# Scaled h in place of the normalised input for the first two gate/up blocks of a two-layer diffusion backbone

## The chip, the cores and the metric

The kernel runs on one core of a Trainium2 chip. The metric is the device time of one execution in microseconds. The core has a matrix engine (TensorE, in the profile PE, its weight loads PEld), VectorE (DVE), ScalarE (ACT), GpSimd (POOL), and a queue engine that issues most loads (SyncE, SP). Matrix products end in PSUM, in 8 banks of 128 x 512 numbers; everything else lies in SBUF.

## The reference

Two layers; in each a half-step feed-forward block, a mixer of three head groups, and a second half-step feed-forward block, on 256 latent and 256 context tokens of 1024 channels. The change touches only the first feed-forward block of the first layer:

```python
def rms_norm(x, g):
    return x * rsqrt(mean(x * x, axis=-1) + EPS) * g
def modulate(n, shift, scale):
    return n * (1 + scale) + shift
def swiglu(x, wg, wu, wd):
    return (silu(x @ wg) * (x @ wu)) @ wd
sh1, sc1, gt1, ... = split(silu(c) @ w_ada[l] + b_ada[l], 9)
h = h + 0.5 * gt1 * swiglu(modulate(rms_norm(h, g_ffn1[l]), sh1, sc1), *ffn1)
```

The context tokens pass through the same weights with their own vectors. For a token with r = 1/rms, the input of the first products is h r m + s, with m = g (1 + scale) and s = shift, both by channel and stream. Its product with a weight column w is therefore r (h m) w + s w: the first factor is one number for each token, the last term one number for each hidden unit and stream.

## The kernel before, in words

Channels lie on the 128 partitions (8 row blocks j), the 512 tokens of both streams along the free dimension. Every product is made of three: activations and weights are each cut into a rounded part and the rest (`xh`/`xl`, `whi`/`wlo`), and `mm3` (L348) adds rounded x rounded, rounded x rest, rest x rounded in PSUM. ScalarE makes a rounded part, VectorE the rest.

A feed-forward block (`ffn`, L429) has 22 hidden blocks of 128 units, each with a gate and an up product (two PSUM banks), in groups of 8, 7 and 7; after each group the down product follows. Weights come as tiles of 128 x 2048 in two raw buffers (`raw`), and are cut by halves of 1024 columns into four buffers each of `whi` and `wlo` (`prefetch`, L321). A half's buffer is free again when its last product has read it.

The first two hidden blocks are made together, in `first_norm` (L140 to 241), while the inputs arrive: h (two loads of 1 MB), the adaLN weights for shift and scale of layer 0 (`wada0`, four quarters q of two halves, 1 MB each, L156), and the weights of blocks 0 and 1 (half tiles, L191). Its steps:

- squares of h on ScalarE, added up on VectorE (L182, L184), then `stats` (L370): sums over the partitions by TensorE, 1/rms in ten small VectorE operations, and its broadcast to all partitions by TensorE; a copy to `rb` (L224)
- for each quarter q: `vectors` (L156, L158), products of the padded activation of c and c_ctx (`cpad`) with the quarter's weights, 512 columns wide, in four column groups of the array; `modulation` (L164 to L176): a copy of the rows, four transposes, a sum, the biases, giving shift `m0` and scale `m1` for two row blocks
- for each row block j: `modulate` (L196 to L203): h times 1/rms on VectorE, scale and shift on ScalarE, rounded part, rest
- `products(j)`: 12 matmuls of 512 columns into the four banks of blocks 0 and 1.

Earlier, `start_ada` (L112) loads c and c_ctx as one row, broadcasts them by eight TensorE instructions (L125) and applies SiLU into `cb`, which the later adaLN sums use: 56 of these in this feed-forward block, made by VectorE (L285) between its other work, each with a 512-KB load (L244).

After that, each hidden block is finished by SiLU of the gate (L456), its product with the up sum (L457), and the cut into `hh` and `hl` (L460, L461), and the PSUM banks are free for the block after next.

The order on each engine is fixed when the program is built: a planner goes through the instructions and lets each engine take, of those whose inputs it believes to be ready, the one that stands first in the program. `issue_after` puts an instruction behind another on its engine. On the chip each engine then runs its list in that order, and loads issued by SP wait in its list until their buffer is free.

## Time and profile before

| | |
|---|---|
| median of 3 runs | 1783.59 us (1782.25 to 1783.96) |
| profiled execution | 1782.73 us, span 1781.0 us |
| TensorE busy | 1730.0 us (97%) |
| VectorE busy | 1144.4 us (64%) |
| ScalarE busy | 647.3 us (36%) |
| GpSimd busy | 97.0 us (5%) |
| read from memory | 249.30 MB, 141 GB/s over the span |

The times in rows of the trace are microseconds from the span's start. A row of the timeline has the start, the busy time, the engine, the line, the operation, output and inputs, and how many instructions were merged into it; in brackets stands how long the engine had been idle and who ended that. Records of matmuls overlap, so the distance between two starts is what one costs, not its length. A row of a group has, behind the bar, the busy time and the mean length in ns. A product of this type on unrounded numbers appears as two instructions.

### The profile page before, as it was taken

The page shows a single profiled execution, that of the slowest core. Times are in us where ns is not written, and L with a number is a line of the kernel's source. Part 1 is how long each engine was busy: PE and PEld are TensorE (multiplying, and loading weights), DVE is VectorE, ACT ScalarE, POOL GpSimd, SP SyncE. Part 2 cuts the span into 40 slices and gives each one's busy share as a digit, 9 for nine tenths or more (in the row PEclk, how much of TensorE's full clock was granted, in tenths as well). Part 3 has the DMA queues.
Part 4 walks back from the last instruction along what each step waited for, and adds up shares of the span by engine and source line. Part 5 has one row for each costly group of instructions (what it writes and reads, how often), then busy time and mean ns, then how long its engine had stood idle before and what let it go on. Part 6 is the DMA issues. An engine that isn't in the chain of part 4 may idle for free.

```text
span 1781.0 us, 24848 instructions
## 1 busy us (share of the span) xinstructions
PE 1730.0 (97%) x9940; PEld 1479.8 (83%) x9940; DVE 1144.4 (64%) x2218; ACT 647.3 (36%) x1053; POOL 97.0 (5%) x130
## 2 busy tenths in 40 slices
PE   7999999999999999999999999999999999989999
PEld 3787888889887688888888898888888898789999
DVE  4777688757657868666676375554543577865554
ACT  4422222234336744212222242222222445744443
POOL 0000000011110010000000110000000311010000
PEclk9999999999999999999999999999999999989999
DMA  7755555532211023544444235534442233135553
GB/s 269 296 195 178 177 178 217 179 101 75 96 57 36 25 107 120 176 165 166 154 178 147 90 122 186 170 134 141 148 141 96 76 118 115 46 109 178 184 184 130
DMA packets 47429, 251.95 MB, mean 141 GB/s; under 512 B 5999, under 2 KB 7233, under 8 KB 29521
## 3 DMA queue, kind: packets, MB, share of 16 engines
q1 hardware_dynamic: 47106, 250.26, 40.5%
q8 instruction: 78, 1.28, 0.3%
q14 instruction: 37, 0.30, 0.1%
q0 software_dynamic: 64, 0.10, 0.0%
q10 hardware_dynamic: 144, 0.01, 0.0%
HBM read 249.30 MB, written 1.05 MB: 141 GB/s over the span
## 4 chain that ended last, share of the span: by engine, by line
PE 88%; DVE 7%; ACT 2%; issue 2%; POOL 1%; DMA 0%; POOLq 0%; ACTq 0%; DVEq 0%
PE mm L350 25%; PE mm L351 25%; PE mm L352 25%; PE mm L627 2%; PE mm L628 2%; PE mm L629 2%; PE aux L836 1%; PE aux L829 1%; DVE wlo L336 1%; POOL acc L368 1%; PE aux L561 1%; PE mm L805 1%; PE aux L774 1%; DVE xl L402 1%; PE aux L387 0%
## 5 line engine op out<-in xcount | busy, mean ns | idle before, releaser
L350 PE MATMUL mm<-xh,whi 128*128 128x512 f32 (+1 forms) x1744 | 606.9, 351 | 6.9 <-ACT xh L201 3.4
L351 PE MATMUL mm<-xl,whi 128*128 128x512 f32 (+1 forms) x1744 | 609.9, 350 | 1.2 <-DVE xl L844 1.2
L352 PE MATMUL mm<-xh,wlo 128*128 128x512 f32 (+1 forms) x1744 | 609.7, 350 | 0.0
L336 DVE TENSOR_TENSOR wlo<-raw,whi 128x1024 fp32r<-128x1024 f32 x324 | 389.5, 1204 | 231.7 <-ACT whi L335 230.2
L335 ACT CAST whi<-raw 128x1024 fp32r<-128x1024 f32 x324 | 332.4, 1027 | 561.5 <-PE mm L351 376.3
L350 PEld LDWEIGHTS mm<-xh,whi 128*128 128x128 f32 x1744 | 332.1, 192 | 52.9 <-ACT xh L201 6.4
L351 PEld LDWEIGHTS mm<-xl,whi 128*128 128x128 f32 x1744 | 333.7, 191 | 45.5 <-issue 1.7
L352 PEld LDWEIGHTS mm<-xh,wlo 128*128 128x128 f32 x1744 | 333.5, 191 | 42.8 <-issue 2.2
L350 PE MATMUL mm<-hh,whi 128*128 128x512 f32 (+1 forms) x788 | 271.3, 344 | 0.0
L351 PE MATMUL mm<-hl,whi 128*128 128x512 f32 (+1 forms) x788 | 270.7, 344 | 0.1
L352 PE MATMUL mm<-hh,wlo 128*128 128x512 f32 (+1 forms) x788 | 270.1, 343 | 0.0
L457 DVE TENSOR_TENSOR gs<-gs,mm 128x512 f32<-128x512 f32 (+1 forms) x88 | 54.7, 621 | 188.1 <-ACT gs L456 149.7
L350 PEld LDWEIGHTS mm<-hh,whi 128*128 128x128 f32 x788 | 149.3, 190 | 19.8 <-issue 2.7
L351 PEld LDWEIGHTS mm<-hl,whi 128*128 128x128 f32 x788 | 149.4, 190 | 18.2 <-DVE hl L461 0.4
L352 PEld LDWEIGHTS mm<-hh,wlo 128*128 128x128 f32 x788 | 149.3, 190 | 17.4
L285 DVE CUSTOM_DVE_ANT_0 ada<-ada,cb 128x1024 f32<-128x1024 f32 x128 | 156.0, 1221 | 2.6 <-DMA ada<-wada 0.6
L407 DVE SCALAR_TENSOR_TENSOR h<-mm,mod,h 128x256 f32<-128x256 f32 x216 | 98.5, 479 | 84.3 <-PE mm L352 83.7
L456 ACT ACTIVATE gs<-mm 128x512 f32<-128x512 f32 (+1 forms) x88 | 48.0, 545 | 276.7 <-PE mm L352 272.8
L368 POOL TENSOR_TENSOR acc<-acc,sq 128x256 f32<-128x256 f32 x63 | 58.2, 932 | 1227.2 <-ACT sq L367 1226.0
L285 DVE CUSTOM_DVE_ANT_0 prod<-ada,cb 128x1024 f32<-128x1024 f32 x96 | 117.0, 1219 | 0.0
L627 PE MATMUL mm<-whi,xh 128*128 128x256 f32 x336 | 97.4, 290 | 0.0
L628 PE MATMUL mm<-wlo,xh 128*128 128x256 f32 x336 | 96.8, 288 | 0.0
(176 smaller groups left out, 1438.3 us busy)
## 6 DMA issues: line engine op xcount, KB each, us to landing
raw<-wgu SPq DMA_DIRECT2D x86, 1024.0 KB, 4.8
ada<-wada SPq DMA_DIRECT2D x128, 512.0 KB, 3.9
raw<-wd SPq DMA_DIRECT2D x32, 896.0 KB, 4.6
raw<-wd SPq DMA_DIRECT2D x16, 1024.0 KB, 4.9
raw<-win SPq DMA_DIRECT2D x12, 1024.0 KB, 5.0
a<-wada SPq DMA_DIRECT2D x8, 1024.0 KB, 4.9
raw<-wout SPq DMA_DIRECT2D x8, 1024.0 KB, 4.9
raw<-why SPq DMA_DIRECT2D x6, 1024.0 KB, 4.8
```

Source lines behind the costliest of these rows:

```text
L285: nc.vector.tensor_tensor_reduce(out=prod, in0=w, in1=self.cb[:, s], scale=1.0, scalar=0.0, op0=ALU.mult, op1=ALU.add, accum_out=m[:, s, j ...
L335: nc.scalar.copy(hi[:, :n], raw)
L336: nc.vector.tensor_tensor(out=lo[:, :n], in0=raw, in1=hi[:, :n].bitcast(F32), op=ALU.subtract)
L350: t.matmul(out, whi, xhi, start=start, stop=False)
L351: t.matmul(out, whi, xlo, start=False, stop=False)
L352: t.matmul(out, wlo, xhi, start=False, stop=stop)
L368: nc.gpsimd.tensor_tensor(out=self.acc[s], in0=self.acc[s], in1=sq, op=ALU.add)
L407: return self.nc.vector.scalar_tensor_tensor(out=self.h[:, j, cols], in0=ps[:, c0:c0 + SEQ], scalar=self.mod(l, ch, s, j), in1=self.h[:, j ...
L456: nc.scalar.activation(gs[:, :n], pg[:, :n], AF.Silu)
L457: nc.vector.tensor_tensor(out=gs[:, :n], in0=gs[:, :n], in1=pu[:, :n], op=ALU.mult)
L627: nc.tensor.matmul(out, self.xh[:, kk, t], hi[:, w], start=kk == 0 and i == 0, stop=False)
L628: nc.tensor.matmul(out, self.xh[:, kk, t], lo[:, w], start=False, stop=False)
```

## The change

`first_norm` no longer waits for the root mean square before the products of blocks 0 and 1. It loads the scale half of the first quarter's adaLN weights first (`vectors(1, 0)`), then half of h and the first halves of the weights, and multiplies h by m alone (`gained`), cut into `uh` and `ul`; these go into the products. The squares come behind the second and fourth row block's products, the statistics behind the sixth. Then the shift halves follow; s is cut into two parts (`sh`), and `shifted(j)` multiplies it with the weights of blocks 0 and 1, 8 small matmuls for each row block into a bank of its own (`pb`), added up into `bias`. The ordinary modulation of all row blocks (`modulate`) comes last, for block 2 and those behind it. Blocks 0 and 1 are finished with `rb` and `bias`. `cb` is made by one broadcast load and one activation at the end. The scratch tiles of squares and modulation now lie in the three buffers of the adaLN weights' tag (`ada`), and the pool `first` is open until block 1 is finished.

```diff
-        crow = self.main.tile([P, 2048], F32, tag="raw", name="raw", bufs=2)[0:1].rearrange("p (s d) -> p s d", s=2)
-        nc.sync.dma_start(crow, a["cc"])
-                nc.tensor.matmul(pt, self.ones[0:1, :], crow[:, s, q * 512:(q + 1) * 512], start=True, stop=True)
-                nc.scalar.activation(self.cb[:, s, q * 512:(q + 1) * 512], pt, AF.Silu)
...
+        def vectors(c, q):
+            pt = self.ps("aux")
+            for half in range(2):
+                w = pool.tile([P, 4, 256], F32, tag="a0", name="a0", bufs=4)
+                nc.sync.dma_start(w, a["wada0"][q, half].rearrange("p (g c k) -> p g c k", g=4, c=2)[:, :, c])
+                for g in range(4):
+                    nc.tensor.matmul(pt[g * 32:(g + 1) * 32, :256], cpad[:, half * 4 + g], w[:, g], start=half == 0, stop=half == 1)
+            return pt
...
+        def gained(j):
+            for s in range(2):
+                cols = slice(s * SEQ, (s + 1) * SEQ)
+                nc.scalar.activation(uh[j][:, cols], self.h[:, j, cols], AF.Identity, scale=m1[:, s, j:j + 1])
+                v.scalar_tensor_tensor(out=ul[j][:, cols], in0=self.h[:, j, cols], scalar=m1[:, s, j:j + 1],
+                                       in1=uh[j][:, cols].bitcast(F32), op0=ALU.mult, op1=ALU.subtract)
...
+        def shifted(j):
+            for k in range(4):
+                hi, lo = weight(j, k // 2, k % 2)
+                nc.tensor.matmul(pb[:, 4 * k:4 * k + 4], hi, sh[:, j].rearrange("p w s -> p (w s)"), start=j == 0 and k == 0, stop=False)
+                nc.tensor.matmul(pb[:, 4 * k:4 * k + 2], lo, sh[:, j, 0], start=False, stop=j == ND - 1 and k == 3)
+
+        parts = vectors(1, 0)
+        inputs(0)
+        weights(0)
+        for q in range(4):
+            modulation(1, q, parts)
+            if q == 0:
+                self.prefetch(2, 2)
+            for j in (2 * q, 2 * q + 1):
+                gained(j)
+            if q < 3:
+                parts = vectors(1, q + 1)
+            if q == 0:
+                inputs(1)
+            elif q == 1:
+                weights(1)
+            elif q == 2:
+                parts0 = vectors(0, 0)
+            for j in (2 * q, 2 * q + 1):
+                products(j)
+            if q in (0, 1):
+                squares(q)
+            elif q == 2:
+                v.tensor_tensor(out=accs[0], in0=accs[0], in1=accs[1], op=ALU.add)
+                rbp, _ = self.stats((0, 1), accs[:1])
+                nc.scalar.copy(rb, rbp)
+        pb = self.ps("aux")
+        for q in range(4):
+            modulation(0, q, parts0)
+            if q == 0:
+                self.prefetch(3, 4)
+            if q < 3:
+                parts0 = vectors(0, q + 1)
+            for j in (2 * q, 2 * q + 1):
+                shifted(j)
+            for j in (2 * q, 2 * q + 1):
+                modulate(j)
+        v.tensor_reduce(out=bias, in_=pb[:, :16].rearrange("p (k w s) -> p k s w", k=4, w=2), axis=AX.X, op=ALU.add)
+        nc.sync.dma_start(self.cb, a["cc"].partition_broadcast(P))
+        nc.scalar.activation(self.cb, self.cb, AF.Silu)
...
+                    if first and b < 2:
+                        up = pool.tile([P, 512], F32, tag="gs", name="up")
+                        nc.vector.tensor_tensor(out=gs, in0=pg, in1=rb, op=ALU.mult)
+                        nc.vector.tensor_tensor(out=up, in0=pu, in1=rb, op=ALU.mult)
+                        for s in range(2):
+                            cols = slice(s * SEQ, (s + 1) * SEQ)
+                            nc.scalar.activation(gs[:, cols], gs[:, cols], AF.Silu, bias=bias[:, 2 * b, s:s + 1])
+                            nc.vector.scalar_tensor_tensor(out=gs[:, cols], in0=up[:, cols], scalar=bias[:, 2 * b + 1, s:s + 1],
+                                                           in1=gs[:, cols], op0=ALU.add, op1=ALU.mult)
```

## Rows read from the trace of the kernel before

**Rows 1.** The page: TensorE's busy time, and the chain that ended last.

```profile
PE 1730.0 (97%) x9940; PEld 1479.8 (83%) x9940; DVE 1144.4 (64%) x2218; ACT 647.3 (36%) x1053; POOL 97.0 (5%) x130
...
PE 88%; DVE 7%; ACT 2%; issue 2%; POOL 1%; DMA 0%; POOLq 0%; ACTq 0%; DVEq 0%
```

**Rows 2.** Timeline of TensorE: first product of the first blocks, products at block 2's start.

```profile
27.40 1.20 PE L350 MATMUL mm<-xh,whi 128*128 128x512 f32 x4 [2.50 <-ACT xh L201]
...
59.60 0.39 PE L350 MATMUL mm<-xh,whi 128*128 128x512 f32 x1
...
60.28 0.39 PE L350 MATMUL mm<-xh,whi 128*128 128x512 f32 x1
```

**Rows 3.** Windows: stretch and length, busy time by engine, PEclk, DMA share, GB/s.

```profile
2.00:4.00 2.00, 1.29 (x2) 0.80 (x3) 0.00 (x0) 0.43 (x1) 1.07 (x3) 1.00 0.92 239
...
4.00:16.00 12.00, 8.27 (x18) 2.38 (x17) 4.57 (x8) 6.64 (x13) 0.00 (x0) 1.00 1.02 415
27.40:59.85 32.45, 31.54 (x150) 20.20 (x151) 14.40 (x29) 17.61 (x30) 0.00 (x0) 0.95 0.63 238
59.85:70.00 10.15, 10.15 (x46) 8.43 (x45) 10.00 (x16) 3.85 (x6) 0.00 (x0) 1.00 0.83 304
70.00:80.00 10.00, 10.00 (x45) 8.26 (x44) 9.97 (x14) 3.21 (x4) 0.00 (x0) 1.00 0.95 364
```

**Rows 4.** Groups by line and shape, ScalarE and VectorE: busy us, mean ns, idle before.

```profile
L200 ACT ACTIVATE xn<-t,mod 128x256 f32<-128x256 f32 x16 | 8.7, 592 | 5.8 <-DVE mod L176 5.8
...
L201 ACT CAST xh<-xn 128x512 fp32r<-128x512 f32 x8 | 4.9, 611 | 0.1
...
L335 ACT CAST whi<-raw 128x1024 fp32r<-128x1024 f32 x292 | 305.8, 1048 | 549.6 <-PE mm L351 364.5 <-issue 144.1 <-PE mm L629 31.0
...
L851 ACT COPY near<-aux 128x256 f32<-128x256 f32 x6 | 2.3, 376 | 2.0 <-PE aux L836 2.0
...
L336 DVE TENSOR_TENSOR wlo<-raw,whi 128x1024 fp32r<-128x1024 f32 x292 | 359.0, 1231 | 230.5 <-ACT whi L335 229.0 <-PE aux L679 0.8
...
L457 DVE TENSOR_TENSOR gs<-gs,mm 128x512 f32<-128x512 f32 x66 | 45.4, 688 | 172.0 <-ACT gs L456 133.6 <-PE mm L352 38.4
...
L407 DVE SCALAR_TENSOR_TENSOR h<-mm,mod,h 128x256 f32<-128x256 f32 x216 | 98.5, 479 | 84.3 <-PE mm L352 83.7
```

**Rows 5.** DMA issues (count, KB each, us to landing), and the issue of `gain`.

```profile
raw<-wgu SPq DMA_DIRECT2D x4, 512.0 KB, 6.9
...
gain<-gain POOLq DMA_DIRECT2D x1, 24.0 KB, 6.2
...
2.20 0.54 POOL L93 DMA_DIRECT2D gain<-gain  x1
```

**Rows 6.** Timeline of TensorE: vector products at either clock, transposes between two products.

```profile
29.61 1.94 PE L158 MATMUL aux<-a,cpad 128*32 128x512 f32 x8
...
40.68 0.39 PE L350 MATMUL mm<-xh,whi 128*128 128x512 f32 x1
...
41.99 0.50 PE L351 MATMUL mm<-xl,whi 128*128 128x512 f32 x1
...
42.79 0.39 PE L351 MATMUL mm<-xl,whi 128*128 128x512 f32 x1
...
43.38 0.48 PE L352 MATMUL mm<-xh,wlo 128*128 128x512 f32 x1
```

**Rows 7.** Timeline of TensorE: the statistics' sums and broadcast.

```profile
15.54 1.87 PE L378 MATMUL aux<-inv_d,acc 128*128 128x2 f32 x8 [1.51 <-DVE acc L219]
...
20.14 2.04 PE L387 MATMUL aux<-dg,ones 128*128 128x128 f32 x8 [0.87 <-DVE dg L386]
```

**Rows 8.** Timeline of weight loads: the filter's column sums, twelve matmuls of two columns.

```profile
173.43 1.52 PEld L548 LDWEIGHTS aux<-ones,ab 128*128 128x128 f32 x12
174.87 0.73 PEld L561 LDWEIGHTS aux<-pm,dft 128*128 128x128 f32 x4
```

**Rows 9.** Windows: one microsecond at the low clock (columns as in rows 3).

```profile
30.00:31.00 1.00, 1.00 (x8) 0.00 (x0) 0.63 (x2) 0.00 (x0) 0.00 (x0) 0.50 0.00 0
```

More of the change, by code (lines that the diff above doesn't have):

```diff
@@ L117, in start_ada @@
         self.cb = self.main.tile([P, 2, D], F32, name="cb")
-        crow = self.main.tile([P, 2048], F32, tag="raw", name="raw", bufs=2)[0:1].rearrange("p (s d) -> p s d", s=2)
-        nc.sync.dma_start(crow, a["cc"])
         self.ccol = self.const.tile([P, ND, 2], F32, name="ccol")
         nc.scalar.dma_start(self.ccol, a["ccol"])
-        for s in range(2):
-            for q in range(2):
-                pt = self.ps("aux")
-                nc.tensor.matmul(pt, self.ones[0:1, :], crow[:, s, q * 512:(q + 1) * 512], start=True, stop=True)
-                nc.scalar.activation(self.cb[:, s, q * 512:(q + 1) * 512], pt, AF.Silu)
         self.mods = {}
@@ L439, in ffn @@
             early = [(self.ps(), self.ps()) for _ in range(2)]
+            scope = ExitStack()
             if first:
-                self.first_norm(pool, early)
+                rb, bias = self.first_norm(pool, early, scope.enter_context(self.tc.tile_pool(name="first", bufs=3)))
             else:
@@ L462, in ffn @@
                     hid.append((hh, hl))
+                    if b == 1:
+                        scope.close()
                     self.ada(ada_steps, done)
```

175 lines of the change are left out of this document (78 added, 97 removed).

## The prediction

> **What bounds the kernel now.** I read the busy shares and the chain that ended last first. The reader is to see that TensorE is busy for 1730 of 1781 us and holds 88% of the chain [rows 1]: nearly everything after the start is a row of products that nothing interrupts, so the change, which touches only the first two gate/up blocks, is worth what it does to one moment, the start of the third block's products (block 2, counted from 0). Then I read the timeline of TensorE for that moment. The first product on the modulated input starts at 27.40 us; the products of the first two blocks end, and those of block 2 begin, at 59.60; from there they follow each other at (60.28 - 59.60) / 3 = 0.227 us [rows 2]. Last I read the stretch between the two: of 32.45 us TensorE is busy for 31.54 [rows 3]. So once it has started it is full, and the 27.4 us before go mostly into waiting: for the squares, the root mean square and the modulation vectors, in this order.
>
> The profiled execution took 1782.73 us, 1.73 more than its span; the median of the runs is 1783.59, 0.86 above it. I work in the profiled execution and add 0.86 at the end.
>
> **The change part by part.** The products no longer wait for 1/rms and the shift. What decides is a trade: an earlier start against more work for TensorE in a stretch where it is the bound.
>
> *The earlier start.* Before, 2 MB of h and 2 MB of adaLN weights are loaded for the first modulation. After, the first product needs the scale half of the first weights (1 MB), half of h (1 MB), and the first half of block 0's weights (0.5 MB). By 4 us 0.48 MB are in (239 GB/s over 2 us), from there 415 GB/s [rows 3]: the vectors' weights are in at 5.4, h at 7.9, block 0's half at 9.2. The last vector product, a copy of 256 columns (0.38 [rows 4]), two transposes, a sum and two small operations take some 2.5 us to 7.9, but the scale also needs `gain`, which is issued at 2.20 and lands 6.2 us later, at 8.4 [rows 5]. Then ScalarE has two scaled halves of h (0.59 each) and the rounded weights (1.05) to make [rows 4]: 8.6 + 2.2 = 10.8. One or two of the squares (0.61 each, as any pass over 512 columns), whose h is there by then, may stand between. I take 11.5 for the first product; bounds 10.7 (nothing between) and 14.5 (third rival).
>
> *The work from there to block 2.* Products: 4 accumulations x 3 terms x 8 row blocks = 96, as before: 21.8 us. Vector products: before, 5 of the 8 half loads fall behind 27.40; one at the high clock holds TensorE from 40.91 to 41.99, 1.08 us, and at the low clock one took 1.94 [rows 6]. The part that goes with the clock is therefore 0.86, the fixed part 0.22. After, there are 16 loads of 256 instead of 512 columns, and 14 of them come behind the first product. No row has this width: half of everything would be 0.54, half of the part that goes with the columns 0.43 + 0.22 = 0.65, which I take. 14 x 0.65 = 9.1 us (7.6 to 10.5). Transposes: four take 43.38 - 43.02 = 0.36 us [rows 6]; seven groups of two at 0.2: 1.4 us. The mean of squares and its broadcast move behind the first product; they take 1.87 and 2.04 us in the idle stretch ahead of it [rows 7], in a full one I take half, as the vector products show it: 2.0 us.
>
> *The shift's products* are new: 8 x 4 x 2 = 64 matmuls with four or two moving columns, each with a 128 x 128 weight load. The nearest row is the filter's column sum: twelve such loads for two columns from 173.43 to 174.87, 0.12 us each [rows 8]. 64 x 0.12 = 7.7 us; bounds 0.09 (the transposes, 0.36 / 4) and 0.23 (the statistics' column sums, 1.87 / 8 [rows 7]): 5.8 to 14.7 us. The Trainium skill, TensorE: Matmul & The Clock Gate, section Back-to-back issue gap, puts matmuls of so few columns about 25 ns apart, which would make 1.6 us of them and reach the first rival's time. Its section on LDWEIGHTS has 107 ns for 128 columns, and the trace, with 0.12, sides with that one: each of the 64 brings new weights.
>
> *Clock.* Before, the granted clock is 0.50 (1.2 GHz) at 30 us [rows 9]; the stretch pays 2.2 us for that (32.2 less 21.8 products, 6.2 vector products, 1.1 transposes and 0.9 idle). TensorE is as idle before its first product afterwards, so I charge 2.2 again.
>
> Sum without waits: 11.5 + 21.8 + 9.1 + 1.4 + 2.0 + 7.7 + 2.2 = 55.7, 3.9 before 59.6. So of the 15.9 us that the start wins, 12.9 go back as work (2.9 vector products, 0.3 transposes, 2.0 statistics, 7.7 shift), against 0.9 idle that is not in this sum.
>
> *Waits.* ScalarE must still do the ordinary modulation for block 2 (8 x (2 x 0.59 + 0.61) = 14.3 us), now beside 16 scalings (9.4), eight copies (3.0) and the activation over 2048 columns for `cb` (1.05 + 2 x (1.05 - 0.61) = 1.9, an estimate) [rows 4]; it was busy for 17.6 of 32.45 us [rows 3] and becomes the second bound from about 40 us. Modulation can begin only with 1/rms and the first shift vectors, near 42 (the first four rows' products, 10.9 us, and the vector products between them stand ahead of both). Its rows are used by block 2 1.4 us apart (6 x 0.227), less than the 1.8 that ScalarE needs for each. With block 2 beginning near 57 this is just hidden, except for some waits in the chain copy, transpose, scale, product, which now runs eight times instead of four and in which the transposes of a quarter stand behind the products of the one before. I take 2.1 us for all waits; before, 0.9 were left [rows 3]. Less than nothing isn't possible; up to 6 is the second rival.
>
> Block 2 then begins at 57.8 instead of 59.6: 1.8 us gained. Edits at nothing: the eight `cb` matmuls and the one-row load fell into idle time of TensorE. SP issues 16 half loads instead of 8 whole ones, on a queue that waits for buffers; on it the load of block 2's weights stands ahead of the last shift halves and waits for block 0's rounding, done near 25. The 1-MB broadcast for `cb` and the late adaLN fetches (their tiles first hold the squares and the modulation's inputs) have until VectorE reaches the first adaLN sum, and VectorE has other work enough (10.00 of 10.15 us busy from 59.85 on [rows 3]). The two-step finish of blocks 0 and 1 costs VectorE 3 x 0.69 + 2 x 0.48 instead of 2 x 0.69 each [rows 4], 3.3 us in all, in its fullest stretch; it delays adaLN sums, not products. Where that cover is gone, it is in the second rival's price.
>
> One price only a page has. The scale loads have lines of 1 KB instead of 8. The Trainium skill, DMA: Bandwidth & Descriptors, section Why small descriptors are slow, gives some 3 cycles for each packet beside one per 32 bytes, so 35 for 32: 8 MB would take an estimated 1.6 us longer, spread over 40 us in which TensorE is the bound. No run here shows it.
>
> 1782.73 - 1.8 = 1780.9 in the profiled execution, 1781.8 for the median.
>
> **The rivals.** *Faster: the new work is cheap.* If the half-wide vector products cost half (7.6) and a shift product 0.09 (5.8), the first product starts at 10.7 and no wait is left, block 2 begins at 10.7 + 21.8 + 7.6 + 1.4 + 2.0 + 5.8 + 2.2 = 51.5: 8.1 us gained, 1775.5. For it: before, TensorE had only 0.9 us of idle in the stretch [rows 3]. Against: 0.12 is measured, which takes 1.9 of the 8.1. Half-way, 1778.6, is already faster.
>
> *Slower: block 2's weights come late.* The rounded weights have four buffers. Before, block 0's were free after the fourth row's products, and block 2's were cut in time. After, all four stay until the shift's products have read them: block 2's halves can only be cut behind the fourth row's shift, block 3's behind the eighth, and ScalarE does it behind the modulation if the order puts it there: 42 + 14.3 + 1.9 + two copies (0.8) = 59.0, and 1.05 + 1.22 for the rounded weights and their rest [rows 4]: 61.3. The second half follows behind the finish of block 0 on a full VectorE, which adds the 3.3 us from above: 64.6, 5.0 us later than before, 1788.6. It decides if that cut begins later than about 57.3 (59.6 less 2.3). For it: VectorE has no idle from 60 to 80 [rows 3]. Against: the modulation itself waits often enough to let the cut in.
>
> *The start doesn't come forward as the change says.* The four half loads of blocks 0 and 1, 512 KB each, took 6.9 us from issue to landing [rows 5]. If the scale halves do the same, the second, issued near 1.4, is in at 8.3 and not at 5.4, the first product comes at 14.5, block 2 at 60.8: 1.2 slower, 1784.8. The Trainium skill, DMA: Bandwidth & Descriptors, Rules for kernel authors, wants 1 MB or more per transfer, which speaks for this case. Against it, 415 GB/s are reached in a stretch with such half loads in its queue [rows 3].
>
> **How the numbers follow.** What a measurement can tell from no change is 0.2%, 3.6 us: faster is below 1780.0, slower above 1787.2. The forecast has 0.44, its own range 1779 to 1785; cheap work 0.29; late weights 0.20; late start 0.07. From these: faster 0.30 (cheap work and a little of the forecast), within 0.2% 0.45, slower 0.25 (late weights, and most of late starts, where waits are added). The range is 1776 to 1789.5: cheap work up to its last 0.5 us, and late weights with 0.9 for a dearer shift product.
>
> **What would show it.** First product between 10.7 and 13; 64 products of the shift at 0.12; half-wide vector products at 0.65; no TensorE gap above 1.5 us before block 2; block 2's first product near 58 and from there the old spacing. Wrong it is if block 2 begins before 55 or behind 62, if TensorE waits for the weights' cut behind block 2's first product, or if the time moves without that moment moving.

## The result and the profile after

The changed kernel takes 1795.38 us (median of 4 runs, 1795.14 to 1795.66), the kernel before 1783.78 beside it: ratio 1.0063 [1.0046, 1.0081]. It is slower by 11.6 us, outside the range of the prediction (1776 to 1789.5), and the forecast of 1781.8 was wrong. The profiled execution took 1795.66 us with a span of 1793.9, 12.9 longer than before. One execution each of e2 and e5 below fell into a much slower state, and the medians leave these two out.

The page after; TensorE's busy line and the chain answer to [rows 1]:

```profile
PE 1735.6 (97%) x10060; PEld 1492.6 (83%) x10060; DVE 1154.0 (64%) x2253; ACT 654.9 (37%) x1073; POOL 96.8 (5%) x130
...
PE 88%; DVE 6%; ACT 2%; issue 1%; POOL 1%; DMA 1%; SPq 0%; POOLq 0%; ACTq 0%; DVEq 0%
```

The page looks as before; everything lies in the first 76 us. The timeline of TensorE after (start, busy time, line, operation, count, idle before) answers to [rows 2] and [rows 6]:

```profile
13.81 1.94 PE L156 MATMUL aux<-a,cpad 128*32 128x256 f32 x16 [13.81 <-ACT cpad L138]
...
20.39 1.65 PE L386 MATMUL mm<-uh,whi 128*128 128x512 f32 x3
...
23.11 0.63 PE L388 MATMUL mm<-uh,wlo 128*128 128x512 f32 x1
...
23.54 0.63 PE L387 MATMUL mm<-ul,whi 128*128 128x512 f32 x1
...
24.69 0.40 PE L387 MATMUL mm<-ul,whi 128*128 128x512 f32 x1
24.92 0.39 PE L388 MATMUL mm<-uh,wlo 128*128 128x512 f32 x1
...
52.78 0.25 PE L232 MATMUL aux<-sh,whi 128*128 128x4 f32 x1
52.89 0.25 PE L233 MATMUL aux<-sh,wlo 128*128 128x2 f32 x1
...
54.71 1.07 PE L156 MATMUL aux<-a,cpad 128*32 128x256 f32 x16
55.71 0.27 PE L232 MATMUL aux<-sh,whi 128*128 128x4 f32 x1
...
58.50 1.83 PE L156 MATMUL aux<-a,cpad 128*32 128x256 f32 x16
...
61.07 0.35 PE L232 MATMUL aux<-sh,whi 128*128 128x4 f32 x1
61.28 0.35 PE L233 MATMUL aux<-sh,wlo 128*128 128x2 f32 x1
...
64.67 0.79 PE L386 MATMUL mm<-xh,whi 128*128 128x512 f32 x1
...
66.95 0.80 PE L386 MATMUL mm<-xh,whi 128*128 128x512 f32 x1 [1.06 <-DVE up L496]
...
75.93 0.39 PE L386 MATMUL mm<-xh,whi 128*128 128x512 f32 x1
```

The first product comes at 20.39, not at 11.5. A product costs 23.54 - 23.11 = 0.43 us there and 0.23 from 24.4 on. A shift product costs 52.89 - 52.78 = 0.11 us, later 61.28 - 61.07 = 0.21. Block 2 has its first product at 64.67, but runs unbroken only from 75.93, with 15 products done before: as if it had begun at 75.93 - 15 x 0.227 = 72.5. That is 12.9 later than 59.6, the whole difference of the spans.

A mark that all the kernels share is the first down product (of `hh`), which stands behind everything that the change touches. Before, then after:

```profile
124.88 0.39 PE L350 MATMUL mm<-hh,whi 128*128 128x512 f32 x1
```

```profile
137.81 0.39 PE L386 MATMUL mm<-hh,whi 128*128 128x512 f32 x1
```

It comes 12.93 us later. What a kernel wins or loses in the changed stretch can be read from this mark with less scatter than from the times: behind it the work is the same, and yet executions differ there by up to 3 us. The granted clock from 421 to 427 us, for example, is 0.50 in v5's trace and 1.00 in v6's.

Windows after (stretch and length, busy time of PE, PEld, DVE, ACT, POOL, granted clock, DMA share, GB/s) answer to [rows 3] and [rows 9]:

```profile
20.39:24.39 4.00, 4.00 (x9) 3.14 (x10) 3.96 (x12) 3.28 (x8) 0.00 (x0) 1.00 0.97 345
20.39:52.60 32.21, 31.23 (x182) 23.50 (x183) 20.67 (x58) 14.68 (x31) 0.00 (x0) 1.00 0.75 256
52.60:58.70 6.10, 5.63 (x57) 4.54 (x60) 1.99 (x7) 3.47 (x8) 0.00 (x0) 1.00 0.51 208
58.70:70.80 12.10, 10.74 (x53) 8.40 (x46) 6.42 (x17) 9.46 (x15) 0.00 (x0) 0.50 0.15 43
...
52.64:70.81 18.17, 16.34 (x106) 12.94 (x105) 8.41 (x22) 12.93 (x22) 0.00 (x0) 0.67 0.28 99
```

The pair's products take as long as before (32.2 us), the shift follows, and from 58.7 on the granted clock is 0.50, 1.2 GHz. The window from 20.39 reads 1.00 although the products stand 0.43 apart, as they do from 72 to 75 us at 0.50. The trace has no clock record ahead of 24.5 us, so there the spacing is to be believed, not the column.

What held the first product is on ScalarE's timeline after, and in its loads (KB each, us to landing), which answer to [rows 5]:

```profile
1.15 1.28 ACT L193 ACT_TABLE_LOAD   x1 [1.15 <-PEq L1053]
11.60 0.63 ACT L193 ACTIVATE acc<-h 128x512 f32<-128x512 f32 x1 [9.17 <-DMA h<-hT]
12.25 1.28 ACT L138 ACT_TABLE_LOAD   x1
13.54 0.22 ACT L138 ACTIVATE cpad<-ccol 128x16 f32<-128x16 f32 x1
```

```profile
a<-wada SPq DMA_DIRECT2D x16, 512.0 KB, 7.6
h<-hT SPq DMA_DIRECT2D x2, 1024.0 KB, 9.5
raw<-wgu SPq DMA_DIRECT2D x4, 512.0 KB, 9.3
```

The first square stands at the head of ScalarE's list, ahead of the SiLU that makes `cpad`, waits 9.17 us for h, and the SiLU needs a second table load. The first product comes 8.79 us behind the start of this square (11.60 and 20.39), and in the five other kernels that keep this order (e2, e3, e5, e7, e9) 8.78 us behind it: where h lands later, all the rest of the start moves with it. The Trainium skill, ScalarE: Activation LUTs, section What ACT_TABLE_LOAD costs, gives 1283 ns for such a load and 1380 more for a drain; the trace has the 1.28, and no drain: the SiLU starts 0.01 us behind it.

### The profile page after: what moved, and what is told of

Same layout as the page of the kernel before. It is cut to its first block, busy times and chain, and to the rows that moved or that the text cites. A ratio compares the mean times of both kernels' runs of the same rounds, so it can differ in the third digit from the quotient of the medians.

```text
span 1793.9 us, 25164 instructions
## 1 busy us (share of the span) xinstructions
PE 1735.6 (97%) x10060; PEld 1492.6 (83%) x10060; DVE 1154.0 (64%) x2253; ACT 654.9 (37%) x1073; POOL 96.8 (5%) x130
## 4 chain that ended last, share of the span: by engine, by line
PE 88%; DVE 6%; ACT 2%; issue 1%; POOL 1%; DMA 1%; SPq 0%; POOLq 0%; ACTq 0%; DVEq 0%
PE mm L386 25%; PE mm L387 25%; PE mm L388 25%; PE mm L676 2%; PE mm L677 2%; PE mm L678 2%; PE aux L885 1%; PE aux L878 1%; DVE wlo L372 1%; POOL acc L404 1%; PE aux L610 1%; PE mm L854 1%; ACT whi L371 1%; DMA h<-hT 1%; PE aux L823 1%
## 5 line engine op out<-in xcount | busy, mean ns | idle before, releaser
L386 PE MATMUL mm<-xh,whi 128*128 128x512 f32 (+1 forms) x1712 | 596.7, 351 | 4.6 <-ACT xh L436 2.4
L387 PE MATMUL mm<-xl,whi 128*128 128x512 f32 (+1 forms) x1712 | 598.6, 350 | 1.1 <-DVE xl L893 1.1
L388 PE MATMUL mm<-xh,wlo 128*128 128x512 f32 (+1 forms) x1712 | 597.9, 350 | 0.0
L386 PEld LDWEIGHTS mm<-xh,whi 128*128 128x128 f32 x1712 | 327.3, 192 | 48.0 <-ACT xh L436 2.9
L387 PEld LDWEIGHTS mm<-xl,whi 128*128 128x128 f32 x1712 | 328.7, 192 | 41.7 <-DVE xl L893 1.7
L388 PEld LDWEIGHTS mm<-xh,wlo 128*128 128x128 f32 x1712 | 328.7, 192 | 40.2 <-issue 0.5
```

The costliest lines, as they stand in the source:

```text
L386: t.matmul(out, whi, xhi, start=start, stop=False)
L387: t.matmul(out, whi, xlo, start=False, stop=False)
L388: t.matmul(out, wlo, xhi, start=False, stop=stop)
```

## The experiments

All of them (medians in us, with the kernel before measured beside each; last columns from the profiled execution: first product, last product of the pair, block 2's first, and the first down product, 124.88 before):

| kernel | median | before | ratio | first | last | block 2 | down |
|---|---|---|---|---|---|---|---|
| after | 1795.38 | 1783.78 | 1.0063 [1.0046, 1.0081] | 20.39 | 52.41 | 64.67 | 137.81 |
| e1_order | 1795.62 | 1782.95 | 1.0067 [1.0051, 1.0083] | 16.91 | 53.66 | 62.77 | 136.43 |
| e2_no_shift | 1784.95 | 1782.95 | 1.0012 [1.0001, 1.0022] | 19.54 | 51.84 | 61.43 | 128.60 |
| e3_wide_shift | 1787.59 | 1782.95 | 1.0031 [1.0019, 1.0044] | 18.89 | 50.97 | 61.03 | 130.31 |
| e4_interleave | 1792.83 | 1782.95 | 1.0054 [1.0037, 1.0070] | 17.33 | 68.27 | 68.63 | 135.88 |
| e5_weights_move | 1794.83 | 1783.51 | 1.0058 [1.0038, 1.0078] | 19.22 | 51.73 | 69.74 | 137.89 |
| e7_lines | 1793.07 | 1783.51 | 1.0055 [1.0040, 1.0070] | 17.54 | 49.46 | 61.71 | 134.80 |
| e9_chain | 1790.74 | 1782.77 | 1.0041 [1.0028, 1.0054] | 18.67 | 49.68 | 65.08 | 132.59 |
| v5 | 1783.25 | 1783.51 | 1.0002 [0.9992, 1.0011] | 11.34 | 51.66 | 58.23 | 125.72 |
| v6 | 1782.45 | 1782.67 | 0.9996 [0.9986, 1.0007] | 11.37 | 49.10 | 57.43 | 124.23 |
| v6_cold | 1782.72 | 1782.67 | 0.9993 [0.9985, 1.0002] | 11.32 | 49.94 | 58.23 | 125.10 |
| v7 | 1780.80 | 1782.77 | 0.9989 [0.9980, 0.9998] | 11.29 | 49.04 | 56.67 | 123.91 |
| v8 | 1780.19 | 1781.89 | 0.9988 [0.9979, 0.9998] | 11.65 | 49.36 | 52.77 | 123.35 |

**e1_order** puts the squares behind the first quarter's scaling and the weights' cut behind the copy of its rows.

```diff
-                nc.scalar.activation(sq, self.h[:, j], AF.Square)
+                with self.tc.issue_after(getattr(anchor, "ins", anchor)):
+                    nc.scalar.activation(sq, self.h[:, j], AF.Square)
...
-                self.prefetch(2, 2)
+                with self.tc.issue_after(getattr(self.rows, "ins", self.rows)):
+                    self.prefetch(2, 2)
...
+            if q == 0:
+                anchor = self.gain_op
```

> The changed kernel with another order on ScalarE at the start alone: the activation of c first, then the copy of the first vector products, the two weight casts, the scaled h, and only then the squares. In the changed kernel a square stood first; it waited 9.17 us for h (to 11.60), a second table load of 1.28 us followed, and the first product came at 20.39 us. Theory (the order on ScalarE held the start back): the vector products run while h is still on its way, both casts and two scaled halves begin when weights and h are in (near 12), first product at 14.5 to 16; the time falls by 4 to 6 us, to about 1790. Rival (the loads set the start): h and the weights share the queue with 2 MB of vector weights, the second quarter's weights and the second half of h come no earlier, so what is won at the start is lost as gaps between the first and the third row block: 0 to 2 us. Second rival (what ends the stretch is ScalarE's modulation behind the pair): no change.

The start came 3.5 us forward, short of the 14.5 to 16 expected, and the time stayed. TensorE's timeline and the window of the pair:

```profile
14.42 1.08 PE L156 MATMUL aux<-a,cpad 128*32 128x256 f32 x8 [4.87 <-DMA a<-wada]
...
44.17 1.13 PE L427 MATMUL aux<-dg,ones 128*128 128x128 f32 x8 [2.72 <-DVE dg L426]
```

```profile
16.90:53.90 37.00, 33.12 (x189) 24.60 (x186) 20.20 (x56) 16.87 (x33) 0.00 (x0) 0.95 0.83 287
```

What holds the first product now are loads: TensorE's list has the second quarter's vector products ahead of it, which wait 4.87 us for their weights. The pair's stretch grew from 32.2 to 37.0 us, 3.9 of it idle: no product stands any more between the statistics' sums (40.50) and their broadcast, and TensorE waits 2.72 us for VectorE between them. So of the 3.5 us, 1.4 are left at the first down product, and none that the time shows; the theory that an earlier start would be worth most of what it moved has fallen.

**e2_no_shift** leaves out the shift's products, with a bias of zero.

```diff
-                shifted(j)
-            for j in (2 * q, 2 * q + 1):
                 modulate(j)
-        v.tensor_reduce(out=bias, in_=pb[:, :16].rearrange("p (k w s) -> p k s w", k=4, w=2), axis=AX.X, op=ALU.add)
+        nc.gpsimd.memset(bias, 0.0)
```

> The changed kernel without the 64 products of the shift; the bias of blocks 0 and 1 is set to zero, so this part of the computation is left out. The vector products for the shift, the transposes and the modulation stay. In the changed kernel the third block's products run without a break from 75.93 us, as if they had begun at 72.5. Theory (the small products cost their own time and, by the low clock they bring with them, that of what follows): 64 x 0.111 = 7.1 us, another 32 x 0.102 = 3.3 for those at the low clock, some 3.0 for 15 products of the third block at the low clock: 10 to 13 us faster, 1783 to 1785. Rival (the modulation of the rows on ScalarE and VectorE is the bound, and the small products only fill its waits): the last row's rounded part comes at 72 us now and cannot come before about 66, so 3 to 6 us faster, and TensorE idles between the third block's rows. Second rival (the clock falls because of the idle time, not because of the small products): 7 us faster, and the granted clock is still 0.50 around 60 to 75 us.

**e3_wide_shift** gives each shift product 256 moving columns, the same four (for the rest of the weights too) again and again.

```diff
-                nc.tensor.matmul(pb[:, 4 * k:4 * k + 4], hi, sh[:, j].rearrange("p w s -> p (w s)"), start=j == 0 and k == 0, stop=False)
-                nc.tensor.matmul(pb[:, 4 * k:4 * k + 2], lo, sh[:, j, 0], start=False, stop=j == ND - 1 and k == 3)
+                wide = sh[:, j:j + 1].rearrange("p o w s -> p o (w s)").to_broadcast([P, 64, 4])
+                nc.tensor.matmul(pb[:, :256], hi, wide, start=j == 0 and k == 0, stop=False)
+                nc.tensor.matmul(pb[:, :256], lo, wide, start=False, stop=j == ND - 1 and k == 3)
```

> The changed kernel with every product of the shift made 256 columns wide: the four columns of the shift are read 64 times over, and all go into the same 256 columns of the bank, so the sums of the four row groups are mixed and the bias is not that of the reference. Same count of matmuls, same weight loads, same waits ahead of them. Theory (the clock falls because TensorE moves almost no columns in these products): the granted clock stays at 1.00 from 52 to 80 us, all 64 products cost 0.11 to 0.12 us, and the time falls by 4 to 7 us. Rival (the clock falls because TensorE waits between the groups, 0.3 to 1 us each): clock at 0.50 from about 58.7 us as in the changed kernel, the products cost 0.21 to 0.24 there, time the same or up to 3 us longer.

The two are read together. Timeline of TensorE and windows of e2_no_shift:

```profile
60.86 0.69 PE L164 MATMUL aux<-ident,rows 128*128 128x128 f32 x2 [3.63 <-ACT rows L161]
```

```profile
58.00:60.00 2.00, 0.00 (x0) 0.00 (x0) 0.20 (x2) 2.00 (x6) 0.00 (x0) 0.60 0.97 332
60.00:62.00 2.00, 1.14 (x3) 0.79 (x4) 1.92 (x4) 2.00 (x5) 0.00 (x0) 0.50 0.92 366
```

The same of e3_wide_shift:

```profile
61.59 0.27 PE L233 MATMUL aux<-sh,whi 128*128 128x256 f32 x1
61.70 0.27 PE L234 MATMUL aux<-sh,wlo 128*128 128x256 f32 x1
```

```profile
51.00:80.00 29.00, 26.20 (x171) 21.20 (x170) 21.76 (x45) 20.92 (x34) 0.00 (x0) 1.00 0.58 209
```

256 columns cost the same 0.11 us as four, and the clock stays at 1.00 from 51 to 80 us, although TensorE is idle for 2.80 of them; after the change it had fallen behind 0.47 us of idle time (52.60 to 58.70). So it was the products of four columns, the first two groups of which TensorE had issued without a gap, that let the clock fall. The time falls by nearly 8 us, 7.5 at the first down product, but 1.5 of these lie in the start of this execution (18.89). Two of the eight runs took 1792.4 us, and no trace was kept of them.

Leaving the shift's products out (e2) takes 9.2 us off the first down product (10.4 by the medians, where 10 to 13 were expected) and leaves 3.7 of the loss. The clock falls all the same, now behind idle time, and block 2 still isn't earlier than 61.43: TensorE waits for the copies of the vector rows, which stand behind the modulation on a ScalarE that is busy for 2.00 of 2.00 us. That chain is the second bound, 1.8 us later than block 2 before, with the shift for nothing.

**e4_interleave** puts each quarter's shift behind its products, so that only the modulation is left at the end.

```diff
-            elif q == 2:
-                parts0 = vectors(0, 0)
+            parts0 = vectors(0, q)
             for j in (2 * q, 2 * q + 1):
                 products(j)
+            modulation(0, q, parts0)
+            for j in (2 * q, 2 * q + 1):
+                shifted(j)
```

> The changed kernel with the shift's weights of each quarter loaded and multiplied next to the scale's, and its 16 small products placed behind the wide products of that quarter; all the modulation comes after the pair. Same work in all. Theory (a long row of small products with waits between the groups, behind the pair, costs the clock and exposes the chain copy, transpose, sum, shift of every quarter): the chains are hidden by wide products, the clock stays at 1.00 behind the start, the third block runs without a break from 61 to 64 instead of 72.5: 8 to 11 us faster, 1784 to 1787. Rival (the 64 products and 16 vector products are simply work for TensorE): it gives back only the waits, 1 to 3 us. Second rival (ScalarE becomes the bound: 8 x 1.8 us of modulation now all behind the statistics): the third block's rows come 1.8 us apart with gaps on TensorE, 4 to 6 us faster.

The theory failed on both counts. Timeline of TensorE and windows:

```profile
28.02 0.24 PE L232 MATMUL aux<-sh,whi 128*128 128x4 f32 x1 [2.48 <-DVE sh L174]
```

```profile
30.00:35.00 5.00, 5.00 (x27) 3.02 (x27) 3.58 (x9) 2.64 (x5) 0.00 (x0) 0.50 0.21 62
```

Behind a wait of 2.48 us for the shift and sixteen small products, all that followed ran at 0.50 for 5 us; which of the two brought the low clock here, this run doesn't separate.

**e5_weights_move** exchanges the operands: the shift's four columns are loaded and the weights move, 32 matmuls of 256 columns and one small transposition at the end.

```diff
-            for k in range(4):
-                hi, lo = weight(j, k // 2, k % 2)
...
+            for b in range(2):
+                for part in range(2):
+                    w = hl[2 * (j // 4) + b][part][:, j % 4 * 256:j % 4 * 256 + 256]
+                    nc.tensor.matmul(pb[:4, b * 256:(b + 1) * 256], sh[:, j].rearrange("p w s -> p (w s)"), w,
+                                     start=j == 0 and b == 0 and part == 0, stop=j == ND - 1 and b == 1 and part == 1)
```

> The changed kernel with the operands of the shift's products swapped: the four columns of the shift are loaded into the array and the weights move through it, 256 columns at a time, 32 matmuls instead of 64; their sums lie on four partitions and are turned by four transposes at the end. Same place, same waits ahead of them. Theory (the few moving columns took the clock down): 32 x 0.11 = 3.5 us, clock 1.00 from 52 to 80 us; what is left is the wait for ScalarE's copies behind the modulation, which the kernel without these products showed, so about the time of that one, 1785 to 1788. Rival (the clock follows how much of the array works, and here only four of its columns do): clock 0.50 from about 58 us, 0.21 us each, 1789 to 1792. Second rival (loading few columns and moving many takes a hold of TensorE that the wide form did not show): over 0.2 us each at the high clock.

Half of the shift's work is gone, and nothing is won. Timeline of TensorE, then of ScalarE:

```profile
59.28 0.69 PE L164 MATMUL aux<-ident,rows 128*128 128x128 f32 x2 [3.98 <-ACT rows L161]
...
63.52 0.41 PE L233 MATMUL aux<-wlo,sh 128*4 128x256 f32 x1
63.73 0.41 PE L233 MATMUL aux<-whi,sh 128*4 128x256 f32 x1
```

```profile
54.58 1.91 ACT L279 ACTIVATE cb<-cb 128x2048 f32<-128x2048 f32 x1 [4.18 <-DMA cb<-cc]
```

ScalarE waits 4.18 us for the load of `cb`, makes it (1.91 us) and modulates before it copies the rows that TensorE waits for; the wait of 3.98 us brings the low clock, and then these products cost 0.21 too.

**e9_chain** is e5 with ScalarE's copies ahead of the modulation and `cb` last; the order of every engine but SP is written out for this stretch.

```diff
+            if q:
+                modulate(q - 1)
+            if q < 3:
+                rows = copy(parts0)
             for j in (2 * q, 2 * q + 1):
                 shifted(j)
...
+        with self.tc.issue_after(getattr(self.copied, "ins", self.copied)):
+            nc.scalar.activation(self.cb, self.cb, AF.Silu)
```

> The kernel with the moving weights (label e5_weights_move, 1795 us: no gain from half the shift's work, because TensorE waited 3.98, 0.49, 0.34, 0.84 and 1.30 us in the chain behind the pair and the clock fell) with one more change: on ScalarE the copy of each quarter's shift vectors stands ahead of the modulation of the rows before, not behind it, one row of modulation stands between two copies, and the activation for the adaLN sums comes behind all modulation. Same work. Theory (ScalarE's order in that chain is what makes TensorE wait, and the wait takes the clock down): no wait above 1 us between 52 and 60 us, clock 1.00 to the end of the chain, third block's first product at 58 to 61, its rows then no faster than ScalarE's 1.8 us each: 1784 to 1788 us. Rival (the amount of work on ScalarE, not its order, is the bound): the third block's last rows come as late as before, at 72, and the time falls by 2 us at most, 1793 or above.

It took 4.1 us off e5 (1790.74 to 1794.83; of their ratios 0.17%), 5.3 at the first down product, between theory and rival: the order on ScalarE is a cause (copies and `cb` together, which this run doesn't separate), but five waits of 0.7 to 2.3 us are left in the chain, and the clock is 0.50 from 56 to 68 in the windows:

```profile
56.00:68.00 12.00, 8.81 (x41) 4.89 (x34) 8.82 (x22) 7.13 (x15) 0.00 (x0) 0.50 0.65 221
```

**e7_lines** lays the scale and shift halves out one behind the other, so that a load has lines of 4 KB, not 1.

```diff
-                nc.sync.dma_start(w, a["wada0"][q, half].rearrange("p (g c k) -> p g c k", g=4, c=2)[:, :, c])
+                nc.sync.dma_start(w, a["wada0"][q, c, half].rearrange("p (g k) -> p g k", g=4))
```

> The changed kernel with the first adaLN weights laid out so that a scale or shift half of a quarter is read in lines of 4 KB instead of 1 KB; nothing else differs. Theory (the loads at the start are slow because five of them share the queue, not because of their lines): the half loads take 7 to 7.6 us from issue to landing as before, and the time stays within 1 us of the changed kernel. Rival (short lines cost bandwidth): the half loads land in 5 to 6 us, the first product comes at 18 instead of 20.4, and the time falls by 1.5 to 3 us.

Its loads by the DMA view:

```profile
a<-wada SPq DMA_DIRECT2D x16, 512.0 KB, 6.3
h<-hT SPq DMA_DIRECT2D x2, 1024.0 KB, 7.1
raw<-wgu SPq DMA_DIRECT2D x4, 512.0 KB, 7.9
```

The first square on ScalarE:

```profile
8.76 0.63 ACT L193 ACTIVATE acc<-h 128x512 f32<-128x512 f32 x1 [6.30 <-DMA h<-hT]
```

They land 1.3, 2.4 and 1.4 us sooner than after the change, and the first product comes at 17.54, 8.78 behind that square. But e2, e3, e5 and e9, whose lines are still short and whose start is unchanged, have 6.3 to 7.2, 7.7 to 8.6 and 8.5 to 8.8, with first products from 18.67 to 19.54: executions scatter, and 0 to 1.5 us are left for the lines. The first down product comes 3.0 us sooner than after the change, nearly all of it (2.85) in the start; the time is not to be told from after's (the intervals overlap). The Trainium skill, DMA: Bandwidth & Descriptors, section Why small descriptors are slow, has a fixed cost for each packet, from which the prediction estimated 1.6 us for all the loads. It points the same way; these runs can't put a number on it.

**v5** writes the order of every engine out by hand: h in quarters, SiLU first on ScalarE, long lines, shift products of e5 in two groups of four row blocks, the first beside the last quarter's products.

```diff
+        last = {}
+        for i in self.nc.cur_bb.bb.instructions[start:]:
+            if i.engine in last:
+                self.tc.add_manual_dep(i, last[i.engine].name, mybir.DependencyInfo(mybir.DependencyClass.NoSync, mybir.DependencyReason.DATA), reason="order")
+            last[i.engine] = i
```

> All findings in one kernel. The order of the instructions of the first phase is written out for each engine: on ScalarE copy, cast, scaled h, with the squares behind them; on TensorE the vector products and transposes of the next quarter stand between the products of the one before. h is loaded by quarters, the adaLN weights in lines of 4 KB, the first product needs 2.5 MB instead of 3. The shift is loaded into the array and the weights move, between the last quarter's products as far as the vectors are there; the statistics stand in the last quarter, the modulation begins there; the activation for the adaLN sums comes behind it. Theory (order and clock were what the change lost): first product at 12.5 to 15, TensorE without gaps over 0.5 us and at full clock from about 18, third block from 50 to 54 instead of 59.6 before and 72.5 after the change: 1774 to 1779 us. Rival (the loads set the pace: 8 MB of vectors, 2 of h and 2 of weights at 375 GB/s): gaps ahead of the second and third quarter, 1779 to 1783. Second rival (ScalarE's modulation, 8 x 1.8 us from about 41 us, is the bound): third block in steps of 1.8 us, 1779 to 1782.

The timeline of TensorE and a window:

```profile
11.34 2.16 PE L241 MATMUL mm<-uh,whi 128*128 128x512 f32 x4 [2.06 <-ACT uh L210]
```

```profile
51.60:58.20 6.60, 3.21 (x24) 1.79 (x23) 5.47 (x13) 6.26 (x13) 0.00 (x0) 1.00 0.92 297
```

The first product comes at 11.34, where the prediction put it, and the loss of 11.6 us is gone, but the theory's 1774 to 1779 us are not reached; what is left is ScalarE's chain ahead of block 2, 6.26 of 6.60 us busy.

**v6** draws the last quarter's work together and warms TensorE up with 24 matmuls without use; **v6_cold** is v6 without those.

```diff
+        keep(14)
         rows = vectors(wv[1, 0])
+        keep(2)
         modulation(1, 0, rows)
+        keep(8)
```

> The kernel with the order written out (label v5), with two more changes. First, 24 matmuls of constants run on TensorE ahead of the first product, in time in which it has nothing to do, so that it is not found at the low clock. Second, the last quarter is rearranged: the last two groups of the shift's vector products and their copies come as soon as 1/rms is there, and the first rows of the modulation ahead of the shift's chain. In the kernel before that rearrangement the first product came at 11.34 us, but 10 us of products and vector products ran at the low clock, the pair ended at 51.9, and TensorE then waited for ScalarE: third block from about 58. Theory (clock and ScalarE's order are what is left): first product at 10 to 12 at full clock, pair at its end by 47 to 49, third block from 52 to 55: 1776 to 1780 us. Rival (ScalarE itself, casts, copies and 8 x 1.8 us of modulation behind 1/rms, is the bound): the third block's rows come 1.8 us apart, 1780 to 1783. Second rival (the loads): gaps of TensorE ahead of the second and third quarter, 1779 to 1782.

> The same kernel (label v6) without the 24 matmuls of constants. Theory (the clock is low after idle time whatever comes, and 10 us of work at the start pay for it): granted clock 0.50 from the first product at about 11.3 to about 17, the third block 2.5 to 3.5 us later than with them, time 2.5 to 3.5 us longer. Rival (ScalarE bounds the end of the stretch): no difference, since what TensorE loses at the start it would otherwise have waited at the end.

Both times are those of the kernel before, above what v6's theory had, and their intervals overlap. The warm-up brought the pair's last product from 49.94 to 49.10, and in the profiled executions these 0.8 us are still there at the first down product (125.10 and 124.23); 2.5 to 3.5 were expected, and the medians can't tell 0.8.

**v7** changes the order of these two in the last quarter (the second halves of the shift ahead of the weights' cut, block 2's products behind the modulation).

```diff
+        begin(3)
+        self.prefetch(4, 6)
+        modulate(2)
         rest(2)
         step(p, 4)
+        modulate(3)
+        for j in range(4, ND):
+            shifted(j)
```

> The kernel with the order written out, warm-up included (label v6, first product near 12 us, pair done at 49.4), with the end of its list put right: there TensorE stood idle from 49.4 to 53 and again up to 58.9, because VectorE took the rests of the third block's weights (2.4 us) ahead of the small operations that make the shift, and ScalarE the casts ahead of the next rows. Now the sums of the last two groups come first, two rows more of the modulation are started ahead of the casts, and the casts of the fourth block and the activations that finish blocks 0 and 1 come behind the modulation. Theory (what is left is order on VectorE and ScalarE): third block's first product at 51 to 54, no gap of TensorE above 1 us behind it: 3 to 6 us below the kernel before the change, 1777 to 1780. Rival (ScalarE's 14 us of modulation behind 1/rms bound the stretch whatever the order): first product as early, but its rows 1.8 us apart with gaps, 1780 to 1783. Second rival (what is won here is given back later, where VectorE has less room for the adaLN sums and TensorE waits for them): TensorE full from 52 to 75 us and the time still that of the kernel before.

**v8** is v7 with block 0's two banks read out by VectorE before the last modulation, and the copy of the shift's sums a row earlier on ScalarE.

```diff
+        v.tensor_tensor(out=gs, in0=pts[0][0], in1=rb, op=ALU.mult)
+        v.tensor_tensor(out=up, in0=pts[0][1], in1=rb, op=ALU.mult)
+        self.early = gs, up
```

> The kernel of label v7 (1780.8 us) with one wait taken out. There the pair and the shift's products were done near 51.3 us, but the third block's first product came at 56.67, because the two PSUM banks of block 0 that it writes into were read by VectorE (sums times 1/rms, two operations) only behind its modulation work; the clock fell meanwhile, and nine products ran at half speed. Now these two operations stand directly behind the last product of block 0, between the two rests of the third block's weights, and the copy of the shift's sums stands a row of modulation earlier on ScalarE. Theory (the release of the banks was the last wait): third block's first product at 52 to 54 at full clock, 4 to 6 us below the kernel of label v7 less what ScalarE's 1.8 us per row gives back: 1776 to 1779. Rival (ScalarE's modulation is the bound from here): products of the third block in groups with gaps behind the third row, 1779 to 1781. Second rival (the sums of the adaLN vectors on VectorE are the next bound, since the same work must now fit in less time): TensorE full up to 80 us and a wait later, 1780 to 1782.

These two beat the changed kernel by far and the one before by 0.11 and 0.12%, with intervals that end 0.02% below no change; the first down product comes 0.97 and 1.53 us sooner than before. Both stay above their theories (1777 to 1780 and 1776 to 1779). TensorE's timeline in v7, then in v8, and v8's windows:

```profile
56.67 0.80 PE L508 MATMUL mm<-xh,whi 128*128 128x512 f32 x1 [3.39 <-DVE gs L621]
```

```profile
52.77 0.50 PE L514 MATMUL mm<-xh,whi 128*128 128x512 f32 x1
...
66.63 0.48 PE L514 MATMUL mm<-xh,whi 128*128 128x512 f32 x1 [1.79 <-DVE gs L629]
```

```profile
52.77:64.50 11.73, 11.73 (x48) 8.54 (x48) 8.22 (x13) 9.18 (x16) 0.00 (x0) 1.00 0.68 254
64.40:68.00 3.60, 1.48 (x5) 0.60 (x5) 3.09 (x5) 3.60 (x8) 0.00 (x0) 1.00 0.89 357
68.00:70.00 2.00, 2.00 (x7) 1.56 (x6) 2.00 (x5) 2.00 (x3) 0.00 (x0) 0.56 0.01 2
```

In v7 the product waits 3.39 us for VectorE to release a bank. In v8 block 2 begins at 52.77, 6.8 us before 59.6, and runs at the full clock; the next block then waits for block 1's banks (1.79 us) and for a weight's rest (0.33), 2.1 us idle between 64.4 and 68, and runs at 0.56 behind it. Most of the 6.8 us is given back there: 1.5 are left. VectorE came to that bank only at 65.80, because ScalarE made `cb` (1.92 us from 62.53) ahead of the SiLU of block 0, for which VectorE waited 1.52 us.

## Why the prediction was wrong

Block 2 was put at 57.8 and came, in effect, at 72.5: 14.7 late. By the terms of the sum:

| term | predicted | measured | difference |
|---|---|---|---|
| first product | 11.5 | 20.39 | +8.9 |
| clock | 2.2 | 1.9 at the start, 7.3 at the end | +7.0 |
| waits | 2.1 | 1.0 to 52.6, 1.8 from there | +0.7 |
| transposes | 1.4 | six groups, 2.0 | +0.6 |
| vector products | 14 x 0.65 = 9.1 | 12 x 0.51 = 6.1 | -3.0 |
| shift's products | 64 x 0.12 = 7.7 | 64 x 0.11 = 7.1 | -0.6 |
| statistics | 2.0 | 1.8 | -0.2 |
| not assigned | | | +1.4 |

The measured clock is the spacing above that of the full clock: at the start 4.0 us of products at half speed; at the end 32 shift products x 0.10 = 3.3, one group of vector products 1.83 - 1.00 = 0.8, transposes 0.2, and 15 products of block 2 x 0.20 = 3.0.

*The earlier start* failed first, by 8.9 us, in two places. Its bounds were 10.7 and 14.5. One is the loads: "415 GB/s from 4 us", taken in the order of their issue, had h in at 7.9, and it landed at 11.6 (issued at 2.13, 9.5 us), 3.7 late. By then some 3.2 MB had been moved (189 GB/s from 2 to 4 us, 372 from 4 to 11.6; an estimate from these windows), where the sum needed 2.1: the loads issued behind h were under way beside it. The other is ScalarE's list: it began with a square, which the sum allowed only between the scaled halves, so that the SiLU and the whole chain of the scale vectors began behind h. From h to the first product the sum had 3.6 us (7.9 to 11.5); it was 8.8 in all six kernels with this order, 5.2 more. The eight `cb` matmuls and their SiLU, an edit costed at nothing, had stood there before. That their going is why the planner put a square first is argued, not tested. With the SiLU first, and nothing else changed but the place of the weights' cut, e1 begins at 16.91, 7.0 us behind its h (9.9): so ScalarE's order alone gave 1.8 of the 5.2, and behind it ScalarE and TensorE wait for the weights' loads. v5 begins at 11.34, but changes order, loads and lines at once. The third rival, a late start, came true in its condition (the scale halves took 7.6 us, where it had 6.9), and the start was late by three times its 3.0 us, with ScalarE's order on top. Nor would the step mended alone have saved the forecast (e1).

*Clock* failed with "so I charge 2.2 again". The charge for the start was near (1.9). None was made for the end: the sum took each matmul's time at the high level, where 64 products of four columns brought the low one, for half of themselves and for block 2's first 15 products (e3). Where they are gone, waits of 2.35 and 3.63 us bring it too (e2).

*Waits* failed in its words "just hidden", though its size was nearly right. With the shift's products hiding it the chain of copy, transposition, shift and modulation cost 1.8 us from 52.6 to 70.8; where they are cheap or gone, the chain shows itself (e2, e5), with the load of `cb`, an edit costed at nothing, in it (4.18 us of ScalarE in e5), and behind it the release of the banks (v7, v8), which I had costed at nothing under "delays adaLN sums, not products". v5 had the forecast's start and cheaper shift products, and still block 2 came at 58.23, near the 57.8, but not by the sum's terms (TensorE is idle for 4.9 us from 11.34 on, where the sum had 2.1), and the time was 1783.25: no gain that can be told.

One sum in the prediction doesn't hold, without deciding anything: the 6.2 us of vector products before are four at 1.08 and one at 1.94, so 0.86 of the price of the low clock stands there and not in the 2.2.

*Late weights*: block 2's first product came at 64.67 with the weights' halves cut just before it, as that rival has it. But the chain above ended at the same time, and in e5 the first halves were cut at 59.65 and 62.17 and block 2 began at 69.74, behind waits for copies; it was not what decided. *Cheap work* needed a short chain behind it: its vector products were in fact cheaper than its 7.6, and v8, with half as many shift products, nearly has its 51.5 for block 2 (52.77), yet the time it forecast, 1775.5, did not follow, as the banks came next.

What stays open: how much the long lines give; why h lands anywhere from 9.9 to 11.6 us in kernels whose loads are the same; 1.4 us of the sum; and whether block 1's banks, freed early as block 0's, would turn v8's 6.8 us into time. That was not tried.

## What to carry to other kernels

Whoever moves work ahead of a wait should write down each engine's list as the planner will make it, above all its first instruction (here the start hung on one square), and ask which loads it waits for once that is put right. A run of matmuls with a handful of moving columns is to be priced twice, by its own spacing and by the clock of what follows; padding their columns cost no time here (e3, whose sums are not the reference's). And when the first bound in a full stretch is taken away, look for the chain that it had hidden (here ScalarE's copies, then the banks' release) before the gain is counted.

## What the runs showed of the hardware

A matmul that brings new 128 x 128 weights cost 0.11 us with 2, 4 or 256 moving columns at the full clock, and 0.21 with four at 0.50. The granted clock fell to 0.50 behind products of four columns with 0.47 us idle among them (after) and behind idle times of 3.63 and 3.98 us (e2, e5), and stayed at 1.00 with 256 columns and 2.80 us idle (e3). The view's clock column read 1.00 over 4.0 us in which products ran at half speed, ahead of the trace's first clock record. A load of 1 MB of h took 9.5 us from its issue, behind 1 MB of other loads, and 5.5 as the first large load before: at the measured 189 and 372 GB/s some 3.2 MB had been moved when the 2.1 MB up to h were in, so a landing is not worked out from the bytes ahead and the rate alone.
